# A hybrid mixer and mixture-of-experts layer: context tokens loaded earlier, a fixed expert order, late experts added into the residual stream, choices summed from the last blocks on

## The chip, the cores and the metric

The kernel runs on one core of a Trainium2 chip. The metric is the device time of one execution in microseconds (us); the time before is the median of three runs. A core has a matrix engine (TensorE, PE in the rows), a vector engine (DVE), an activation engine (ACT), a general one (POOL), a sequencer that only issues transfers (SP), and 16 DMA engines between the chip's memory (HBM) and the on-chip memory.

## The reference

One layer over 512 latent tokens of width 1024 with 256 context tokens ahead of them: a modulated RMSNorm, one projection, latent attention beside a recurrent block, an output projection, and then the part in which most of the time goes, a mixture of 64 experts. Each token picks 8 of them.

```python
def routed_experts(h, eidx, w, exp_w_gate, exp_w_up, exp_w_down):
    ...
    def body(acc, blk):
        tok_b, w_b, e_b = blk
        y = swiglu(h[tok_b], exp_w_gate[e_b], exp_w_up[e_b], exp_w_down[e_b])
        return acc.at[tok_b].add(y * w_b[:, None]), None
    ...
h_lat = modulate(rmsnorm(x, norm_mix_g[l]), sh1, sc1)
h_ctx = modulate(rmsnorm(ctx, norm_mix_g[l]), csh1, csc1)
...
x = x + g1 * (y_lat @ w_out[l])
...
x = x + g2 * (routed_experts(f_lat, ...) + swiglu(f_lat, sh_w_gate, sh_w_up, sh_w_down))
return rmsnorm(x, final_norm_g)
```

All is in float32. An expert has gate and up weights of 1024x256 and down weights of 256x1024, 1 MiB each; all 64 are used.

## The kernel before

**Prologue (to about 70 us).** SP issues the loads of this stage in the order of the code: the latent tokens (`load_x`, 4 of 512 KB), the key-value columns of the input projection (`wkv`), the first two modulation weights (`load_wm1(0)`), the context tokens (2 of 512 KB), the query columns (`wq`), and more weights. Each token tile is squared on ACT (line 295), gets its reciprocal root on DVE (lines 152 to 162, nine small operations) and is scaled there (line 299), then PE transposes it (`pt`, line 326) and DVE or ACT copies the result out. The modulation's rows come from PE (`pm`, line 311), and the first projection (`pkv`, line 362) needs the transposed tokens, modulated and split into a high and a low part (`hH`, `hL`).

**Recurrent block, attention (to about 332 us), output projection.** After the modulation rows are saved (`mrd<-modrow`) and two parts of the output weights are loaded (`wor`), SP has nothing to issue until attention is done.

**Routing and shared expert (332 to 440 us).** PE and DVE compute the router's logits, each token's 8 choices, and the place of every (token, choice) row in its expert's list. Beside that PE works off the shared expert in four token tiles: `sgu` (gate and up), `smul` (DVE), `sdn` (transposes `pst`, down products `psd`, then two DVE operations with `g2b` and the residual `x1`, and a store into the buffer `acc` in HBM). A scheduler sets the order of this stage by priorities.

**Expert blocks (440 to 1043 us).** The experts have ranks by the number of their tokens, and each rank has a capacity in units of 32 rows, 183 units in all. The list `order` (built at line 1090 on by a rule with `NTAIL` and `LEAD`) is cut into 46 blocks of up to 128 rows, so that one block can hold units of several experts. A block is a chain: `stage_sel` and `stage_gather` (three to four blocks ahead: its token rows, by an indirect DMA of POOL), `stage_trans` (PE `tr`, a copy `hT`), `stage_gu` (PE `gu`, 7 us), `stage_at`, `stage_down` (PE `dn`, 3.7 us, in a PSUM tile of which there is one; then `y` on DVE, line 1406, and an indirect DMA of POOL that scatters the rows into `yd`, a buffer in HBM with one row for each token and choice). PE's order here is written by hand: `gu` of a block, `tr` of the next, `at`, `dn`.

The weights come by SP: `load_upto` issues gate, up and down of the n-th expert in the list when the last block of the expert six places ahead is done, since there are six slots for each (`g0` to `g5` for gate and up, `d0` to `d5` for down); at most `OUTST` = 3 loads are in flight. Before the routing is known only the first `NF` = 3 experts can be loaded.

**End (1043 to 1113 us).** A loop over experts that overflow their capacity (no pass here) begins and ends with all engines waiting for each other. Then `fgb` (a gain) and 16 loads `yl<-yd` of 1 MB each bring the 8 choices of all tokens back. For each of four token tiles PE adds four choices (`fs`, with an identity matrix), DVE adds the other four and then PE's sum to the residual in `xs` (lines 1550 and 1551), ACT squares (`jk`), a root follows, and the scaled tile is stored. `fsum`, `fsq`, `frs` and `fout` are these steps.

## Time and profile before

| | |
|---|---|
| median of 3 runs | 1115.37 us (1114.18 to 1116.23) |
| the profiled execution | 1114.81 us |
| its span, first to last instruction | 1112.8 us |
| mean granted clock of TensorE | 0.962 |
| busy: PE / DVE / ACT / POOL | 996.2 / 484.3 / 255.7 / 223.4 us |
| HBM read / written | 293.31 / 30.29 MB |

The profile is one execution. Busy times do not count waits; a row of the timeline shows in brackets how long its engine stood idle before it and what ended that. The clock of TensorE is given as a share of its full 2.4 GHz. Numbers of a load or of a queue are of that queue alone; the DMA share of a window is that of all 16 engines.

### The profile page before, as it was taken

To read this page: it belongs to the slowest core of one execution; us is meant where nothing else is said; L and a number is where in the kernel's file an instruction comes from. 1 tells how busy PE (TensorE), PEld (TensorE's weight loads), DVE (VectorE), ACT (ScalarE), POOL (GpSimd) and SP (SyncE) were. 2 spreads that over 40 slices of the span, in tenths; PEclk is the share of its full clock that TensorE was granted. 3 is DMA by queue.
4 is the path that set the end of the run, shared out by engine and by line. 5 is a ranking of instruction groups with operands and counts; after the bars stand their busy time and mean duration, and the time that the engine had idled before them with its cause. 6 is when DMAs were issued, how large, how long until landed. Compare 5 with 4: busy or idle time off the path is not lost. (4 is left out here: it accounts for less than half of the span.)

```text
span 1112.8 us, 17435 instructions
## 1 busy us (share of the span) xinstructions
PE 996.2 (90%) x6813; PEld 515.6 (46%) x6813; DVE 484.3 (44%) x1064; ACT 255.7 (23%) x468; POOL 223.4 (20%) x219
## 2 busy tenths in 40 slices
PE   3899989799989998999999999999999999995482
PEld 2687654567779853443443344333333333331131
DVE  5527594988765865223222232222322223220065
ACT  3433545756661210011000110000100001000011
POOL 3382341346100001111111111111111111110001
PEclk9899999889999999999999999999999999997797
DMA  9834644200009543999999898989879999989694
GB/s 294 266 96 154 206 161 133 77 1 1 1 2 365 226 195 132 416 394 417 419 409 360 333 390 346 395 323 399 339 289 401 399 413 414 399 319 414 251 421 186
DMA packets 75404, 310.34 MB, mean 279 GB/s; under 512 B 12747, under 2 KB 31234, under 8 KB 48442
## 3 DMA queue, kind: packets, MB, share of 16 engines
q1 hardware_dynamic: 60412, 271.79, 63.2%
q0 software_dynamic: 13936, 34.26, 8.1%
q10 hardware_dynamic: 974, 3.17, 0.8%
q8 instruction: 54, 0.88, 0.3%
q14 instruction: 28, 0.23, 0.1%
HBM read 293.31 MB, written 30.29 MB: 291 GB/s over the span
## 5 line engine op out<-in xcount | busy, mean ns | idle before, releaser
L1382 PE MATMUL gu<-wgu,hT 128*32 128x512 f32 (+2 forms) x2160 | 333.0, 597 | 11.1 <-DMA wgu<-in_exp_w_up_dram 10.4
L1382 PEld LDWEIGHTS gu<-wgu,hT 128*32 128x32 f32 (+2 forms) x2160 | 105.4, 120 | 230.2 <-issue 225.9
L1403 PE MATMUL dn<-wd,aT 128*32 128x512 f32 (+2 forms) x1080 | 169.1, 596 | 16.6 <-ACT aT L124 15.4
L1385 DVE TENSOR_TENSOR act<-act,gu 128x256 f32<-128x256 f32 (+1 forms) x46 | 19.4, 421 | 297.8 <-ACT act L1384 297.8
L1384 ACT ACTIVATE act<-gu 128x256 f32<-128x256 f32 (+1 forms) x46 | 17.7, 385 | 511.7 <-PE gu L1382 511.7
L1332 POOL DMA_INDIRECT hg<-h2d,bix x46 | 47.6, 1034 | 425.9 <-issue 310.4
L1406 DVE SCALAR_TENSOR_TENSOR y<-dn,bw,g2b 128x1024 f32<-128x1024 f32 (+1 forms) x46 | 59.0, 1283 | 138.2 <-PE dn L1403 138.2
L1403 PEld LDWEIGHTS dn<-wd,aT 128*32 128x32 f32 (+2 forms) x1080 | 48.7, 119 | 100.8 <-issue 78.8
L1407 POOL DMA_INDIRECT yd<-y,biy x46 | 46.8, 1017 | 191.9 <-DVE y L1406 182.5
L1370 PEld LDWEIGHTS tr<-ident,hg 128*128 128x128 f32 (+1 forms) x368 | 39.9, 141 | 37.1 <-issue 34.1
L1370 PE MATMUL tr<-ident,hg 128*128 128x128 f32 (+1 forms) x368 | 49.7, 278 | 1.3 <-DVE tb L1084 1.3
L1548 PE MATMUL fs<-yl,ident 128*128 128x512 f32 x64 | 32.1, 654 | 20.3 <-DMA yl<-yd 18.1
L829 PE MATMUL pTr<-ident,P 128*128 128x128 f32 x192 | 30.7, 300 | 9.8 <-DVE P L820 7.7
L1306 DVE TENSOR_TENSOR sv<-iot,posR 128x256 bf16<-128x256 f32 (+3 forms) x93 | 37.1, 411 | 0.0
L812 DVE TENSOR_REDUCE nm<-pS 128x1 f32<-128x768 f32 x32 | 30.3, 951 | 11.2 <-PE pS L810 10.8
L124 ACT COPY PT<-pTr 128x384 f32<-128x384 f32 x64 | 28.0, 482 | 29.0 <-PE pTr L829 28.7
L124 ACT COPY hT<-tr 128x512 f32<-128x512 f32 (+1 forms) x46 | 26.9, 584 | 34.0 <-PE tr L1370 32.5
L840 PE MATMUL po<-PT,vsb 128*64 128x128 f32 x384 | 30.8, 299 | 1.7 <-ACT PT L124 1.7
L454 PE MATMUL pmx<-wm,csil 128*32 128x512 f32 x128 | 31.9, 606 | 0.0
L124 DVE COPY hT<-tr 128x512 f32<-128x512 f32 (+1 forms) x46 | 31.3, 680 | 0.0
L1548 PEld LDWEIGHTS fs<-yl,ident 128*128 128x128 f32 x64 | 12.7, 208 | 39.8 <-DMA yl<-yd 20.4
L829 PEld LDWEIGHTS pTr<-ident,P 128*128 128x128 f32 x192 | 24.1, 153 | 14.8 <-issue 7.7
(473 smaller groups left out, 1472.9 us busy)
## 6 DMA issues: line engine op xcount, KB each, us to landing
wgu<-in_exp_w_gate_dram SPq DMA_DIRECT2D x64, 1024.0 KB
wgu<-in_exp_w_up_dram SPq DMA_DIRECT2D x64, 1024.0 KB
wd<-in_exp_w_down_dram SPq DMA_DIRECT2D x64, 1024.0 KB
...
```

The source lines that it names most:

```text
L124: (e.copy if e is ACT else e.tensor_copy)(dst, src)
L454: PE.matmul(pm[32 * g:32 * g + 32, :], csil[:, kk, :], wmp[n, g // 2][:, (g % 2) * 512:(g % 2 + 1) * 512], start=(kk == 0), stop=(kk == KT ...
L829: PE.transpose(p[:, j * P:(j + 1) * P], Pm[u][:, k * P:(k + 1) * P], ident)
L840: PE.matmul(po[i][64 * hh:64 * hh + 64, t * P:(t + 1) * P], vsb[:, k, 2 * i + hh, :], PTt[i, t, hh][:, k, :], start=(k == 0), stop=(k == N ...
L1306: DVE.tensor_tensor(sv[:, :, c:c + w], iot[:, u:u + w][:, None, :].to_broadcast([P, NT, w]), col_[:, :, None].to_broadcast([P, NT, w]), op ...
L1332: POOL.indirect_dma_start(out=b.hg[0:m], out_offset=None, in_=h2d, in_offset=bass.IndirectOffsetOnAxis(ap=b.ix[0:m, :1], axis=0), bounds_c ...
L1370: PE.transpose(p[:, i * m:(i + 1) * m], b.hg[0:m, (i0 + i) * P:(i0 + i + 1) * P], ident[0:m, 0:m])
L1382: PE.matmul(p[c:c + w, :], b.hT[:, k, c:c + w], wg[n][:, :, k, :], start=(k == 0), stop=(k == KT - 1))
L1403: PE.matmul(p[c:c + w, n0:n0 + 512], b.aT[:, k, c:c + w], wd_[n][:, k, n0:n0 + 512], start=(k == 0), stop=(k == 1))
L1406: DVE.scalar_tensor_tensor(y[0:m], p[0:m], b.w[0:m], g2b[0:m], op0=OP.mult, op1=OP.mult)
L1407: ins = POOL.indirect_dma_start(out=yd, out_offset=bass.IndirectOffsetOnAxis(ap=b.iy[0:m, :1], axis=0), in_=y[0:m], in_offset=None, bounds ...
L1548: PE.matmul(p[:, n0:n0 + 512], ident, yl[t, k][:, n0:n0 + 512], start=(k == 0), stop=(k == 3))
```

## The change

- The context tokens are loaded directly behind the latent tokens, and `wkv` comes behind the first modulation weights.
- The list of experts is a table, `ORDER`. The last `LATE` = 5 of them (full 128 rows each) have a block of their own. In the same number of blocks (46) the last two of before held units of four and of three experts.
- The rows of these five blocks aren't written into `yd` but added into `acc` by the DMA itself; `acc` has 128 rows more, into which rows without a token are sent (`spad`). `yd` (16.8 MB) and these rows (0.5 MB) are filled with zeros by five transfers behind the loads of `wor`.
- The shared expert's parts are in an order written out by hand, `sgu(2)` and `sgu(3)` among the routing's products. `x1` and `wgu_s` change their buffers, so that slot `g2` comes free after `sgu(3)`, and `load_upto(NW - 2)` stands right behind it.
- DVE's order is written by hand from the first expert block on.
- The 16 loads `yl<-yd` are issued as slots come free in the last blocks (`sum_loads`). The first five of DVE's additions stand between `y` of block 44 and that of block 45, the rest behind the last `y`; PE adds four choices of the token tiles 1 to 3 (`fs`, in the tiles of `dn`, `tr` and `gu`). After the loop `acc` is loaded (`ya`, 4 of 512 KB) and added once for each token tile.

The diff, cut to its core (the removed `yload` issued the 16 loads behind the loop):

```diff
--- before.py
+++ after.py
@@ -75,9 +75,15 @@
...
-NTAIL = 8
...
+ORDER = [61, 62, 63, 35, 60, 48, 52, 21, 43, 38, 9, 50, 34, 2, 46, 28,
...
+LATE = 5
 OUTST = 3
...
 L0 = 2
...
@@ -112,7 +118,7 @@
...
+    acc = dram.tile([S + P, D], F32, name="acc")
...
@@ -264,7 +270,7 @@
...
-    wkv = load_win(C_KV, 160)
+    load_x(ctx[0], 2)
     wm1 = {}
...
@@ -274,7 +280,7 @@
...
     load_wm1(0)
-    load_x(ctx[0], 2)
+    wkv = load_win(C_KV, 160)
     wq = load_win(0, 256)
     for c in range(1, 4):
         load_wm1(c)
@@ -782,6 +788,12 @@
...
+    zt = modrow.rearrange("p a b -> p (a b)")
+    POOL.memset(zt, 0.0)
+    SP.dma_start(acc[S:S + P, :], zt)
+    for t in range(NT):
+        SP.dma_start(yd.rearrange("(t p k) f -> t p k f", p=P, k=TOPK)[t], zt[:, None, :].to_broadcast([P, TOPK, D]))
...
@@ -933,7 +945,7 @@
...
-    x1 = pW1.tile([P, NT, D], F32, tag="g2", name="x1")
+    x1 = pW1.tile([P, NT, D], F32, tag="g4", name="x1")
...
@@ -958,7 +970,7 @@
...
-    wgu_s = pW1.tile([P, 2, KT, FF], F32, tag="g4", name="wgu_s")
+    wgu_s = pW1.tile([P, 2, KT, FF], F32, tag="g2", name="wgu_s")
...
@@ -1056,47 +1070,48 @@
...
-    @prio("sgu")
-    def sgu(t):
-        p = sgp[t] = psx("psg")
-        for k in range(KT):
+    def sgu(t, k0=0, k1=KT):
+        if k0 == 0:
+            sgp[t] = psx("psg")
+        p = sgp[t]
+        for k in range(k0, k1):
             PE.matmul(p, h2T[:, k, t * P:(t + 1) * P], wgu_s[:, :, k, :], start=(k == 0), stop=(k == KT - 1))
-        sga[t] = et("act", "sg")
+        if k1 < KT:
+            return
...
-    @prio("sdn")
-    def sdn(t):
+    sgT = {}
+    def sdt(t):
...
-        p = pw("psd")
-        for n in range(2):
...
+    def sdp(t):
+        tb = et("y", "tb")
+        x_ = x1[:, t]
+        for n0 in range(0, D, 512):
+            p = psx("psd")
             for k in range(2):
-                PE.matmul(p[:, n * 512:(n + 1) * 512], sgT[:, k, :], wd_s[:, k, n * 512:(n + 1) * 512],
-                          start=(k == 0), stop=(k == 1))
-        tb = et("y", "tb")
-        DVE.tensor_tensor(tb, p, g2b, op=OP.mult)
-        DVE.tensor_tensor(tb, tb, x1[:, t], op=OP.add)
-        ACT.dma_start(acc[t * P:(t + 1) * P, :], tb)
+                PE.matmul(p, sgT[t][:, k, :], wd_s[:, k, n0:n0 + 512], start=(k == 0), stop=(k == 1))
+            DVE.tensor_tensor(tb[:, n0:n0 + 512], p, g2b[:, n0:n0 + 512], op=OP.mult)
+        DVE.tensor_tensor(x_, tb, x_, op=OP.add)
+        ACT.dma_start(acc[t * P:(t + 1) * P, :], x_)
...
-    order = [E - NF + j for j in range(NF)]
...
-    lead = LEAD
-    while left:
-        r = left.pop(0 if lead <= 0 else -1)
-        order.append(r)
-        lead += caps[r] * 0.092 - (8.1 + caps[r] * 0.019)
-    order += range(E - NF - NTAIL, E - NF)
-    GS, NW = (5, 0, 1, 2, 3, 4), 6
+    order = ORDER
+    GS, DS, NW = (5, 0, 1, 2, 3, 4), (0, 1, 2, 3, 5, 4), 6
...
@@ -1123,10 +1138,14 @@
...
     for n, r in enumerate(order):
+        if n >= E - LATE:
+            assert caps[r] <= P
+            at = 0
         for u in range(0, caps[r], 32):
...
@@ -1142,11 +1161,13 @@
...
+    for b in blocks[-LATE:]:
+        b.late = True
...
-        loads += [(n, "g") for n in new] + [(n, "d") for n in new]
+        loads += [(n, w) for n in new for w in ("dg" if n == NF else "gd")]
...
@@ -1180,6 +1201,8 @@
...
     logits(2)
+    st_M = ExitStack()
+    st_M.enter_context(tc.manual_schedule(engines={mybir.EngineType.PE}))
     sgu(0)
...
@@ -1234,6 +1257,8 @@
...
+    smul(1)
+    sgu(2, 0, 4)
...
@@ -1269,12 +1294,16 @@
...
+    sgu(2, 4, 6)
...
+    sgu(2, 6, 8)
...
@@ -1325,8 +1354,12 @@
...
+        if b.late:
+            DVE.tensor_scalar(b.iy[0:m], tk[0:m], float(FAR), spad[0:m], op0=OP.add, op1=OP.min)
+        else:
...
@@ -1334,30 +1367,32 @@
...
     LA = 3
-    smul(1)
+    sgu(3)
+    st_O.close()
+    st_E2 = ExitStack()
+    pE2 = st_E2.enter_context(tc.tile_pool(name="pE2", bufs=1))
+    load_upto(NW - 2)
+    smul(2)
     stage_sel(blocks[0])
     stage_sel(blocks[1])
-    sdn(0)
-    sgu(2)
+    smul(3)
+    sdt(0)
     stage_gather(blocks[0], pn("ix0"))
-    smul(2)
-    sdn(1)
+    sdt(1)
+    sdp(0)
     stage_gather(blocks[1], pn("ix1"))
     stage_sel(blocks[2])
-    sgu(3)
-    load_upto(NW - 2)
-    smul(3)
+    sdt(2)
+    sdp(1)
     stage_gather(blocks[2], pn("ix2"))
-    sdn(2)
-    sdn(3)
-    st_O.close()
+    sdt(3)
+    sdp(2)
+    sdp(3)
...
@@ -1404,13 +1439,16 @@
...
         DVE.scalar_tensor_tensor(y[0:m], p[0:m], b.w[0:m], g2b[0:m], op0=OP.mult, op1=OP.mult)
+        if b.late:
+            POOL.indirect_dma_start(out=acc, out_offset=bass.IndirectOffsetOnAxis(ap=b.iy[0:m, :1], axis=0),
+                                    in_=y[0:m], in_offset=None, bounds_check=S + P - 1, oob_is_err=True, compute_op=OP.add)
...
@@ -1459,8 +1497,42 @@
...
+    st_M.enter_context(tc.manual_schedule(engines={mybir.EngineType.DVE}))
+    ydv = yd.rearrange("(t p k) f -> t p k f", p=P, k=TOPK)
+    pairs = [(t, k) for t in range(NT) for k in range(0, TOPK, 2)]
+    homes = [("d", E - 6)] + [(w, n) for n in range(E - 5, E) for w in "dgh"]
+    yl, rest, place = {}, list(zip(pairs, homes)), {}
+    xs = None
+    def sum_loads(i):
+        nonlocal xs
+        if xs is None and i >= last[E - 6]:
...
+            (t, k), (w, n) = rest.pop(0)
...
+            ins = SP.dma_start(z, ydv[t, :, k:k + 2, :]).ins
+            for y_ in yw:
+                after(ins, y_, "rows of all blocks but the last")
+            yl[t, k] = z
+    def add_pair(t, k, first):
+        x_ = xs[:, t]
+        for j in range(2):
+            if first and j == 0:
+                DVE.tensor_tensor(x_, yl[t, k][:, 0, :], yl[t, k][:, 1, :], op=OP.add)
+            elif not first:
+                DVE.tensor_tensor(x_, x_, yl[t, k][:, j, :], op=OP.add)
...
@@ -1476,14 +1548,31 @@
...
+        if not loads:
+            sum_loads(i)
+        if i == NB - 2:
+            for k in (0, 2, 4):
+                add_pair(0, k, k == 0)
         if i in (10, 12, 14, 16):
             got = next(table)
...
+    for t in range(1, NT):
+        if t == 1:
+            p = pse.tile([P, D], F32, tag="dn", name="fs", bufs=1)
+            fs = [p[:, 0:512], p[:, 512:1024]]
+        else:
+            fs = [pse.tile([P, 512], F32, tag=("gu", "tr")[t % 2], name="fs", bufs=2) for _ in range(2)]
+        for k in range(4):
+            for h in range(2):
+                PE.matmul(fs[h], ident, yl[t, k - k % 2][:, k % 2, h * 512:(h + 1) * 512], start=(k == 0), stop=(k == 3))
+        add_pair(t, 4, True)
+        add_pair(t, 6, False)
+        for h in range(2):
+            x_ = xs[:, t, h * 512:(h + 1) * 512]
+            DVE.tensor_tensor(x_, x_, fs[h], op=OP.add)
     st_M.close()
-
-    xs = pW1.tile([P, NT, D], F32, tag=f"g{GS[(E - 6) % NW]}", name="xs")
-    for t in range(NT):
-        SP.dma_start(xs[:, t], acc[t * P:(t + 1) * P, :])
     n_ov = nc.values_load(nov[0:1, 0:1], min_val=0, max_val=NOV)
...
@@ -1520,35 +1606,14 @@
...
-    def yload(t, k0, n, buf):
...
+    n = E - 5
+    ya = (pW0 if GS[n % NW] < 2 else pW1 if GS[n % NW] < 5 else pW2).tile([P, NT, D], F32, tag=f"g{GS[n % NW]}", name="ya")
+    for t in range(NT):
+        SP.dma_start(ya[:, t], acc[t * P:(t + 1) * P, :])
     @prio("fsum")
     def fsum(t):
-        p = psf.tile([P, D], F32, tag="fs", name="fs", bufs=2)
-        for n0 in range(0, D, 512):
-            for k in range(4):
-                PE.matmul(p[:, n0:n0 + 512], ident, yl[t, k][:, n0:n0 + 512], start=(k == 0), stop=(k == 3))
-        for k in range(4, TOPK):
-            DVE.tensor_tensor(xs[:, t], xs[:, t], yl[t, k], op=OP.add)
-        DVE.tensor_tensor(xs[:, t], xs[:, t], p, op=OP.add)
+        DVE.tensor_tensor(xs[:, t], xs[:, t], ya[:, t], op=OP.add)
...
```

What this does to the instructions, at three places. First SP's issues in the prologue, from the latent tokens on. Before:

```order
L256 DMA xz<-in_x_dram 128x1024 x4
L264 DMA win<-in_w_in_dram 128x8x160
L273 DMA wm_136<-in_w_mod_dram 128x8x256
L273 DMA wm_138<-in_w_mod_dram 128x8x256
L256 DMA xz<-in_ctx_dram 128x1024 x2
L264 DMA win<-in_w_in_dram 128x8x256
L273 DMA wm_145<-in_w_mod_dram 128x8x256
```

And now:

```order
L262 DMA xz<-in_x_dram 128x1024 x4
L262 DMA xz<-in_ctx_dram 128x1024 x2
L279 DMA wm_137<-in_w_mod_dram 128x8x256
L279 DMA wm_139<-in_w_mod_dram 128x8x256
L270 DMA win<-in_w_in_dram 128x8x160
L270 DMA win<-in_w_in_dram 128x8x256
L279 DMA wm_145<-in_w_mod_dram 128x8x256
```

`xz<-in_ctx_dram` went up by three rows, and `wkv` (128x8x160) down by three.

Second PE, from the routing to the first expert block (`psg` are the products of `sgu`, `pst` and `psd` those of the shared expert's second half, `ptr` and `ppr` belong to the routing, `tr` begins block 0). Before, the last rows ahead of block 0:

```order
L1075 MATMUL pst<-ident,sg 128x128
L1063 MATMUL psg<-wgu_s,h2T 128x512
L1075 MATMUL pst<-ident,sg 128x128 x2
L1081 MATMUL psd<-wd_s,sgT 128x512 x4
L1063 MATMUL psg<-wgu_s,h2T 128x512 x2
L1081 MATMUL psd<-wd_s,sgT 128x512 x4
L1063 MATMUL psg<-wgu_s,h2T 128x512 x2
L1075 MATMUL pst<-ident,sg 128x128 x2
L1081 MATMUL psd<-wd_s,sgT 128x512 x4
L1370 MATMUL tr<-ident,hg 128x128 x8
```

And now, rows that end ahead of the first selection of token rows (`ix`):

```order
L1078 MATMUL psg<-wgu_s,h2T 128x512 x2
L1302 MATMUL ptr<-ident,eq 64x128 x4
L1302 MATMUL ptr<-ident,se 64x128 x4
L1078 MATMUL psg<-wgu_s,h2T 128x512 x2
L1309 MATMUL ppr<-perm,sT 128x64 x8
L1078 MATMUL psg<-wgu_s,h2T 128x512 x8
L1096 MATMUL pst<-ident,sg 128x128 x2
```

The last products of `psg` stood among the second half, three rows ahead of block 0; they now stand ahead of the first `pst`.

Third DVE, from the last block but one on. Before, up to the loop:

```order
L1406 SCALAR_TENSOR_TENSOR y<-dn,bw,g2b 128x1024
L1385 TENSOR_TENSOR act<-act,gu 128x256
L124 COPY hT<-tr 128x384
L1406 SCALAR_TENSOR_TENSOR y<-dn,bw,g2b 128x1024
L1385 TENSOR_TENSOR act<-act,gu 96x256
L1406 SCALAR_TENSOR_TENSOR y<-dn,bw,g2b 96x1024
L1489 TENSOR_LOAD nov
```

And now (line 1441 is `y`, line 1420 `act`), up to the additions of token tile 2; those of tile 3 and the loop follow:

```order
L130 COPY hT<-tr 128x512
L1441 SCALAR_TENSOR_TENSOR y<-dn,bw,g2b 128x1024
L1532 TENSOR_TENSOR xs<-yl 128x1024
L1534 TENSOR_TENSOR xs<-xs,yl 128x1024 x4
L1420 TENSOR_TENSOR act<-act,gu 128x256
L1441 SCALAR_TENSOR_TENSOR y<-dn,bw,g2b 128x1024
L1534 TENSOR_TENSOR xs<-xs,yl 128x1024 x2
L1532 TENSOR_TENSOR xs<-yl 128x1024
L1534 TENSOR_TENSOR xs<-xs,yl 128x1024 x2
L1574 TENSOR_TENSOR xs<-xs,fs 128x512 x2
L1532 TENSOR_TENSOR xs<-yl 128x1024
```

The additions of choices, which stood behind the loop, stand ahead of it, five of them ahead of the last `y`; a single addition of `ya` for each token tile is left behind the loop.

## Rows read from the trace of the kernel before

**Rows 1.** Waits of TensorE over the span: line, releaser: us, times, longest us

```profile
PE fs L1548 <- DMA yl<-yd: 18.1, 5, 13.4
PE dn L1403 <- ACT aT L124: 15.4, 46, 0.6
PE pt L326 <- DVE xz L299: 11.5, 3, 4.6
PE gu L1382 <- DMA wgu<-in_exp_w_up_dram: 10.4, 4, 3.6
PE pTr L829 <- DVE ccol L1419: 2.1, 1, 2.1
```

**Rows 2.** Timeline, prologue, SP, DVE, PE: start, us, engine, line, operation [idle before]

```profile
7.79 0.43 SPq L264 DMA_DIRECT2D win<-in_w_in_dram  x1
11.83 2.63 SPq L256 DMA_DIRECT2D xz<-in_ctx_dram  x2
32.18 1.42 DVE L299 TENSOR_SCALAR xz<-xz,rstd 128x1024 f32<-128x1024 f32 x2
33.08 2.73 PE L326 MATMUL pt<-ident,xz 128*128 128x128 f32 x10 [4.64 <-DVE xz L299]
```

**Rows 3.** Timeline, SP around attention

```profile
196.84 1.91 SPq L784 DMA_DIRECT2D wor<-in_w_out_dram  x2
332.84 0.34 SPq L943 DMA_DIRECT2D g1b<-mrd  x1
```

**Rows 4.** Windows, routing: us, busy by engine (x), PEclk, DMA share, GB/s

```profile
405.00:420.00 15.00, 13.92 (x66) 7.08 (x65) 9.78 (x28) 1.82 (x4) 0.00 (x0) 1.00 0.00 0
420.00:440.00 20.00, 16.98 (x57) 7.82 (x55) 11.81 (x23) 1.50 (x4) 4.02 (x3) 1.00 0.32 114
```

**Rows 5.** Timeline, PE, from the shared expert's end into blocks 0 and 1

```profile
439.18 1.09 PE L1370 MATMUL tr<-ident,hg 128*128 128x128 f32 x8 [1.32 <-DVE tb L1084]
441.04 8.82 PE L1382 MATMUL gu<-wgu,hT 128*128 128x512 f32 x16 [0.77 <-DVE hT L124]
455.72 6.60 PE L1382 MATMUL gu<-wgu,hT 128*128 128x512 f32 x15
```

**Rows 6.** Timeline, DVE, line 1406: start of y in blocks 0, 43, 44, 45

```profile
455.49 1.28 DVE L1406 SCALAR_TENSOR_TENSOR y<-dn,bw,g2b 128x1024 f32<-128x1024 f32 x1 [2.77 <-PE dn L1403]
999.10 1.28 DVE L1406 SCALAR_TENSOR_TENSOR y<-dn,bw,g2b 128x1024 f32<-128x1024 f32 x1 [4.22 <-PE dn L1403]
1015.67 1.28 DVE L1406 SCALAR_TENSOR_TENSOR y<-dn,bw,g2b 128x1024 f32<-128x1024 f32 x1 [6.47 <-PE dn L1403]
1042.74 1.28 DVE L1406 SCALAR_TENSOR_TENSOR y<-dn,bw,g2b 96x1024 f32<-96x1024 f32 x1 [4.69 <-PE dn L1403]
```

**Rows 7.** Windows, expert blocks; then the page's row of POOL's DMA queue

```profile
700.00:800.00 100.00, 97.29 (x942) 35.10 (x942) 27.61 (x81) 9.96 (x24) 16.22 (x16) 1.00 0.93 367
1000.00:1030.00 30.00, 18.01 (x110) 5.15 (x113) 2.56 (x4) 1.24 (x3) 1.96 (x2) 0.80 1.01 415
q0 software_dynamic: 13936, 34.26, 8.1%
```

**Rows 8.** Timeline, after the last y: POOL, SP, PE, DVE, ACT

```profile
1044.29 0.95 POOL L1407 DMA_INDIRECT yd<-y,biy  x1 [26.09 <-DVE y L1406]
1049.20 0.34 SPq L1518 DMA_DIRECT2D fgb<-in_final_norm_g_dram  x1
1056.10 11.96 PE L1548 MATMUL fs<-yl,ident 128*128 128x512 f32 x20 [13.42 <-DMA yl<-yd]
1068.57 5.42 PE L1548 MATMUL fs<-yl,ident 128*128 128x512 f32 x12 [0.51 <-DMA yl<-yd]
1092.58 5.00 DVE L1550 TENSOR_TENSOR xs<-xs,yl 128x1024 f32<-128x1024 f32 x4
1097.68 1.22 DVE L1551 TENSOR_TENSOR xs<-xs,fs 128x1024 f32<-128x1024 f32 x1
1102.99 1.15 ACT L1573 ACTIVATE xs<-xs,rf 128x1024 f32<-128x1024 f32 x1 [2.49 <-DVE rf L1566]
```

82 lines of the change are left out of this document (32 added, 50 removed), and 3 rows, old and new, of the table ORDER.

## The prediction, made before the run

> **What bounds the kernel now.** I read TensorE's waits over the whole span first [rows 1]: they add up to little, and the larger ones have a place each. The sum of choices waits 18.1 us for its loads, the down products 15.4 us for a copy that no part of the change touches (46 times a third of a microsecond), the transposes of the prologue 11.5 us for a scaling, the gate products 10.4 us for weights. Then the windows of the expert blocks [rows 7]: PE is busy for 97.29 of 100 us, while the DMA engines have a share of 0.93. So the long middle is PE's, with the loads close behind. Then the starts of `y` [rows 6], one for each block: from block 0 to block 43 they are (999.10 - 455.49) / 43 = 12.64 us apart; the last two are 16.57 and 27.07 us apart. There the DMA share is 1.01 at 415 GB/s, and PE works 18.01 of 30 us [rows 7]: loads bind, since seven experts of few rows (21 MB of weights) fall into two blocks. Last, from the start of the last `y` to the end of the span, 1112.8 - 1042.74 = 70.06 us pass, with loads, additions and stores in turn [rows 8]. So the change is to be judged in five places: prologue, attention, routing, blocks, end.
>
> **A, prologue.** PE waits 4.64 us for the scaled context tokens [rows 2], whose two loads are issued at 11.83, behind `wkv` at 7.79 and two modulation weights. With these loads first, that wait is gone. The modulation weights now have 1 MB of context ahead of them in the place of 0.65 MB of `wkv` (128x8x160 floats), so the modulated latent tokens come 0.4 MB later, about 1 us at 415 GB/s [rows 7]. `wkv` lands about where the context did, and has to be split before the first projection; I take 0.6 us for that. 4.6 - 1.0 - 0.6 = 3.0 us gained. Ends: 4.6 gained, or 2 lost (the whole MB of context, 2.5 us, ahead of the modulation, with nothing gained). Behind it PE is full, so a gain here is passed on.
>
> **B, attention.** DVE's operations on the overflow table, which cost PE 2.1 us in attention [rows 1], move into the blocks, where DVE is busy 27.61 of 100 us [rows 7]. The clearing on POOL is one operation in a stretch in which POOL is mostly idle; I allow 0.6 us. The five transfers that write zeros, 16.8 + 0.5 = 17.3 MB, are issued behind `wor` at about 199 us; SP issues nothing more until 332.84 [rows 3], so they have 134 us and need 129 GB/s of DMA engines that are otherwise idle. Taken as hidden: 1.5 us gained, ends 2 gained and 1 lost. What it costs if that cover is too short is a rival below.
>
> **C, routing to block 0.** In the last stretch ahead of block 0 PE waits 1.32 us for DVE's residual addition and 0.77 us for the copy of block 0, and the first gate products take 8.82 us, where 15 of the 16 of the next block take 6.60 [rows 5] (the whole about 7.04). That is 1.3 + 0.8 + 1.8 = 3.9 us that an order with filled gaps can take back. The hand-written order puts `sgu(2)` and `sgu(3)` where PE would wait for the routing, and so leaves less to fill the gap ahead of the first selection; I keep 3.0. Ends: 5 gained, 1 lost. The first `y` then starts at 455.49 - 7.5 = 448.0.
>
> **D, the blocks.** 45 intervals of 12.64 us are 568.8 us, where 1042.74 - 455.49 = 587.25 us pass now [rows 6]: 18.4 us less, if weights never bind. Whether they bind I worked out by a queue walk: 61 experts with three loads of 1.05 MB at 2.6 us (403 GB/s, a little below the 415 of the saturated window), 34.26 MB of gathers and scatters [rows 7] spread over 46 blocks (0.74 MB or 2.2 us each), a load not before its slot is free, three in flight. For the order of before the walk loses 19 us, all in the last two blocks; the trace shows 16.57 + 27.07 - 2 x 12.64 = 18.4. For the table it loses 6 us, in blocks 17 and 36, where slots come free late; at 2.55 us a load none, at 2.65 us 13. I take 3: D = 18.4 - 3 = 15.4 us gained, ends 20 (blocks a little tighter) and 5. Two things help that the walk has: slot `g2` comes free after `sgu(3)`, so that the DMA engines, which move nothing from 405 to 420 and have a share of 0.32 until 440 [rows 4], start on the fourth expert earlier; and the last five blocks need one expert each. The 16 loads of choices now fall into these blocks: 16.8 MB are 40 us at 415 GB/s, in five blocks of 63 us that have no weights left to load. The last `y` starts at 448.0 + 568.8 + 3 = 1019.8.
>
> **E, the end.** After the last `y` (1.28 us) PE has the sums of three token tiles, 48 records. The first of these needs the PSUM tile that `y` reads. At the upper clock 12 records take 5.42 us [rows 8], 0.45 each: 21.7 us. DVE has in the same time 2 + 3 x 3 additions of 1024 columns at 1.25 and 6 halves, about 17.5 us, and so is covered; the last half, 0.6 us, is not. 1.28 + 21.7 + 0.6 = 23.6. The loop's barrier and the first issue behind it: 2.0 (`fgb` is issued at 1049.20, 4.0 us after POOL was done with its scatter at 1045.24, and most of that is the scatter landing). Then `fgb` (0.5 MB) and four times 0.5 MB of `acc`: from the issue of `fgb` to PE's first sum, behind 1.57 MB, it took 1056.10 - 1049.20 = 6.9 us; 1.05 MB more at 415 GB/s is 2.5, so 9.4. One addition, 1.22. From the end of the last addition, 1098.90, to the end of the span 13.9 us, which stay; and since DVE then does the roots of two tiles and scales two tiles at once, 3.5 more. 23.6 + 2.0 + 9.4 + 1.2 + 13.9 + 3.5 = 53.6, against 70.06: 16.5 us gained. Ends: 21 (no mutual delay of the tiles) and 0 (the 48 records at the clock's lower level, where 20 records at first took 11.96 [rows 8], some 40 us instead of 21.7).
>
> **Sum.** 3.0 + 1.5 + 3.0 + 15.4 + 16.5 = 39.4 us. The profiled execution took 1114.81, so 1075.4; the median lies 0.56 above it: **1076 us**.
>
> **The rivals.** (1) *The loads bind.* At 2.7 us a load, or with 3 us of DMA time a block in place of 2.2, the walk loses 20 to 32 us in blocks 13 to 39 in place of 3: 1093 to 1105. For it: shares of 0.93 to 1.01 [rows 7]. Against it: the same walk with the smaller numbers meets the waits of before. Chance 0.12. The Trainium skill, "DMA: Bandwidth & Descriptors", section "Specifications", names about 358 GB/s as what a core gets from its HBM. By that alone the 226 MB of weights (61 x 3.15), gathers and scatters (34.26) would take 630 us from about 425 on, and 1076 would be about 1118, no gain; the window at 415 GB/s [rows 7] speaks against it, and I give such a result 0.01. (2) *The late additions are a chain.* Each transfer that adds into `acc` has to wait for the one before; if one takes longer than a block of 12.64 us, they pile up, and the loop's barrier waits for the last. The nearest row is a plain scatter, issued at 1044.29 and over before 1049.20 [rows 8], under 5 us. At 20 us the chain ends 5 x 20 = 100 us after the first late `y` at 1019.8 - 4 x 12.64 = 969.2, at 1069 in place of 1043: 26 us more, 1102. Chance 0.04. The skill's same page, section "Rules for kernel authors", says why the chain is needed: an adding DMA reads its target and writes it later, and another write in between is lost. (3) *The zeros outlast attention*, the case on the other side. All that follows at 332.84 needs the same 16 engines: `g1b`, tokens and output weights. Above 129 GB/s nothing is lost; each us behind 332.84 costs up to one; 39.4 us are used up at a finish at 372, that is 17.3 MB in 173 us, 100 GB/s. At 80 GB/s they take 216 us, end at 415, and the time is 1076 + 82 = 1158. Against it: 415 GB/s in a saturated stretch [rows 7]; for it only that no row shows a write of this size from a broadcast source. Chance 0.04. (4) *The context load gains nothing:* A is 0 and the time 1079, inside the range.
>
> **How the numbers follow.** Forecast 0.79, loads 0.12, chain 0.04, zeros 0.04, no gain 0.01. The forecast's own ends, not all at once, give 1058 to 1092. The range holds these and the near half of the loads' case: 1060 to 1096; what lies outside is about 0.2. A measurement of this kernel tells about 0.2% from no change. Faster by more than that: 0.79 + 0.12 + 0.04 = 0.95; the same 0.01; slower 0.04.
>
> **What would show it.** A: TensorE's wait for line 299's scaling falls from 11.5 to under 8. B: the DMA windows between 200 and 250 show the writes, and SP's first issue behind attention is not followed by a longer wait of PE. C: the first `y` near 448. D: starts of `y` 12.6 apart up to the last, and waits for weights of some us near blocks 17 and 36; if the walk is wrong, more of these. E: `fs` behind the last `y` without a wait for loads, and 53 us from that `y` to the end. The prediction is wrong if the intervals between blocks grow to 13 us or more, since 45 of them multiply it.

## The result, and the profile after

The changed kernel took **1076.68 us** (median of 4 runs, 1073.87 to 1082.02) against 1115.8 before (4 runs): a ratio of 0.9653, with a 95% interval from 0.9608 to 0.9698. The forecast was 1076. The profiled execution took 1078.44, its span is 1076.7, so 36.1 us less than the span of before.

The sum agrees because the two large terms held; the small ones in front of them did not. In the two profiled executions the span falls into the parts of the prediction like this (the gains add up to 36.0 us, where 39.4 were forecast):

| part | before | after | gained | predicted |
|---|---|---|---|---|
| A, to the store of the modulation rows (SP) | 196.12 | 196.30 | -0.2 | 3.0 |
| B, from there to the first issue behind attention | 136.72 | 133.77 | 2.9 | 1.5 |
| C, from there to the first `y` | 122.65 | 122.11 | 0.5 | 3.0 |
| D, first `y` to last `y` | 587.25 | 571.76 | 15.5 | 15.4 |
| E, last `y` to the end | 70.06 | 52.76 | 17.3 | 16.5 |

TensorE's waits over the whole span (line, releaser: us, times, longest us) answer to [rows 1]. The wait of `fs` for its loads is gone, that of `gu` for weights has shrunk from 10.4 to 1.4, and that of the prologue's transposes from 11.5 to 7.4, as the prediction asked of A; and yet A brought nothing.

```profile
PE dn L1438 <- ACT aT L130: 16.0, 46, 0.5
PE pt L332 <- DVE xz L305: 7.4, 5, 2.2
PE gu L1417 <- DMA wgu<-in_exp_w_up_dram: 1.4, 1, 1.4
PE fs L1569 <- DVE y L1441: 1.4, 1, 1.4
```

**A.** PE's timeline in the prologue (start, us, operation, idle before), and two windows (us, then busy us and count of PE, PEld, DVE, ACT, POOL, then PEclk, DMA share, GB/s):

```profile
30.80 0.47 PE L368 MATMUL pkv<-hH,wh 128*128 128x512 f32 x1 [0.32 <-ACT hH L394]
33.40 0.58 PE L370 MATMUL pkv<-hH,wh 128*128 128x256 f32 x1 [0.95 <-ACT hH L394]
35.77 0.80 PE L368 MATMUL pkv<-hL,wh 128*128 128x512 f32 x1 [1.00 <-DVE hL L398]
36.58 0.63 PE L368 MATMUL pkv<-hH,wl 128*128 128x512 f32 x1
...
32.00:36.00 4.00, 2.05 (x8) 1.06 (x9) 3.71 (x3) 2.54 (x4) 3.98 (x2) 0.65 1.10 348
36.00:40.00 4.00, 4.00 (x19) 3.06 (x23) 0.96 (x1) 0.00 (x0) 0.00 (x0) 0.50 1.10 348
```

Before, the first of these products and one of the same shape as the last:

```profile
37.98 0.61 PE L362 MATMUL pkv<-hH,wh 128*128 128x512 f32 x1
39.25 0.39 PE L362 MATMUL pkv<-hH,wl 128*128 128x512 f32 x1
```

The first projection (`pkv`) starts at 30.80 where it started at 37.98, seven us earlier. But the projection falls into a stretch in which PE waits for ACT and DVE to split the tokens (0.95 and 1.00 us), and which has a granted clock of 0.65 and then 0.50, its lower level of 1.2 GHz. There a product of 512 columns takes 0.63 us where the same took 0.39 before, at 39 us. Of the seven us 1.4 are left at the first product of the recurrent stage (`pp`, at 72.26 in place of 73.65), and these too are lost by the store of the modulation rows at 196.30. The section on the prediction takes this up.

**B.** SP's issues and the windows of attention, which answer to [rows 3]:

```profile
200.37 23.77 SPq L796 DMA_DIRECT2D yd<-modrow  x4
330.07 0.34 SPq L955 DMA_DIRECT2D g1b<-mrd  x1
...
207.00:240.00 33.00, 28.00 (x166) 21.35 (x165) 31.86 (x43) 20.61 (x40) 20.81 (x12) 0.92 1.02 421
240.00:260.00 20.00, 18.78 (x115) 13.90 (x113) 15.94 (x23) 12.52 (x27) 7.79 (x5) 0.79 0.35 142
```

The zeros go out at 421 GB/s and are done by about 247 (a share of 0.35 of the window from 240 to 260), 83 us ahead of the first load behind attention.

**D.** The starts of `y` on DVE that answer to [rows 6], with blocks 16 and 17 (the second and third row):

```profile
452.18 1.28 DVE L1441 SCALAR_TENSOR_TENSOR y<-dn,bw,g2b 128x1024 f32<-128x1024 f32 x1 [2.46 <-PE dn L1438]
654.53 1.28 DVE L1441 SCALAR_TENSOR_TENSOR y<-dn,bw,g2b 128x1024 f32<-128x1024 f32 x1 [2.60 <-PE dn L1438]
670.26 1.28 DVE L1441 SCALAR_TENSOR_TENSOR y<-dn,bw,g2b 128x1024 f32<-128x1024 f32 x1 [2.69 <-PE dn L1438]
1011.34 1.28 DVE L1441 SCALAR_TENSOR_TENSOR y<-dn,bw,g2b 128x1024 f32<-128x1024 f32 x1 [4.22 <-PE dn L1438]
1023.94 1.28 DVE L1441 SCALAR_TENSOR_TENSOR y<-dn,bw,g2b 128x1024 f32<-128x1024 f32 x1 [4.82 <-PE dn L1438]
```

The intervals are 12.5 to 13.0 us to the very end. One is longer, 15.73 us, that of block 17, which the queue walk had named; block 36, the other one it had named, has 12.75. PE's rows in block 17:

```profile
655.01 1.07 PE L1417 MATMUL gu<-wgu,hT 128*64 128x512 f32 x2
657.46 7.05 PE L1417 MATMUL gu<-wgu,hT 128*64 128x512 f32 x30 [1.38 <-DMA wgu<-in_exp_w_up_dram]
```

Its gate products end 9.5 us after the first began, in place of 7.1, with a wait for weights among them: 2.4 us. The other 0.64 us are products of the overflow table (`pot`, from 654.37 to 655.01), which stand in that block before the change too, where its interval is 13.32 us.

**E.** Behind the last `y`: PE, DVE, SP, and a window of it, to be read beside [rows 8].

```profile
987.13 38.07 SPq L1523 DMA_DIRECT2D yl<-yd  x16
1025.28 20.87 PE L1569 MATMUL fs<-yl,ident 128*128 128x512 f32 x48 [1.38 <-DVE y L1441]
1043.14 1.23 DVE L1532 TENSOR_TENSOR xs<-yl 128x1024 f32<-128x1024 f32 x1 [3.13 <-DMA yl<-yd]
1045.69 2.48 DVE L1534 TENSOR_TENSOR xs<-xs,yl 128x1024 f32<-128x1024 f32 x2 [1.33 <-DMA yl<-yd]
1048.28 1.29 DVE L1574 TENSOR_TENSOR xs<-xs,fs 128x512 f32<-128x512 f32 x2
1051.40 1.94 SPq L1612 DMA_DIRECT2D ya<-acc  x4
1056.72 2.51 DVE L1616 TENSOR_TENSOR xs<-xs,ya 128x1024 f32<-128x1024 f32 x2 [7.16 <-DMA ya<-acc]
1062.75 4.57 DVE L1640 SCALAR_TENSOR_TENSOR xs<-xs,rf,fgb 128x1024 f32<-128x1024 f32 x2
...
1030.00:1040.00 10.00, 10.00 (x25) 4.39 (x24) 7.47 (x9) 0.00 (x0) 0.00 (x0) 1.00 1.03 371
```

PE's 48 records take 20.87 us (21.7 predicted) and end at 1046.15. But DVE waits 3.13 and 1.33 us for the last loads of choices, and its last addition ends at 1049.57: the DMA engines, busy all the time (1.03 at 371 GB/s), end last, not PE. SP began to issue these loads at 987.13 and had issued the last of the 16 at about 1025, behind the last `dn`. The part up to the loop is 25.6 us (23.6 predicted), that behind it is shorter (27.1, 30.0 predicted).

### The profile page after: what moved, and what is told of

Read it like the earlier page. It is cut to its first block, busy times and chain, and to the rows that moved or that the text cites. A ratio compares the mean times of both kernels' runs of the same rounds, so it can differ in the third digit from the quotient of the medians.

```text
span 1076.7 us, 16080 instructions
## 1 busy us (share of the span) xinstructions
PE 978.7 (91%) x6125; PEld 523.5 (49%) x6125; DVE 489.7 (45%) x1062; ACT 255.1 (24%) x468; POOL 234.6 (22%) x221
## 5 line engine op out<-in xcount | busy, mean ns | idle before, releaser
L1417 PE MATMUL gu<-wgu,hT 128*32 128x512 f32 (+3 forms) x1776 | 326.5, 594 | 2.1 <-DMA wgu<-in_exp_w_up_dram 1.4
L1417 PEld LDWEIGHTS gu<-wgu,hT 128*32 128x32 f32 (+3 forms) x1776 | 111.7, 127 | 209.3 <-issue 208.2
L1438 PE MATMUL dn<-wd,aT 128*32 128x512 f32 (+3 forms) x888 | 168.5, 597 | 16.0 <-ACT aT L130 16.0
L1365 POOL DMA_INDIRECT hg<-h2d,bix x46 | 50.4, 1095 | 418.9 <-issue 305.1
L1438 PEld LDWEIGHTS dn<-wd,aT 128*32 128x32 f32 (+3 forms) x888 | 52.1, 127 | 96.8 <-issue 76.2
L1446 POOL DMA_INDIRECT yd<-y,biy x41 | 41.2, 1004 | 138.3 <-DVE y L1441 125.0
L1335 DVE TENSOR_TENSOR sv<-iot,posR 128x256 bf16<-128x256 f32 (+3 forms) x86 | 34.1, 435 | 0.0
L1078 PE MATMUL psg<-wgu_s,h2T 128*128 128x512 f32 x64 | 30.6, 625 | 0.0
L826 ACT ACTIVATE P<-pS,nm 128x768 f32<-128x768 f32 x32 | 29.1, 909 | 4.8 <-DVE nm L824 4.6
```

The costliest lines, as they stand in the source:

```text
L1078: PE.matmul(p, h2T[:, k, t * P:(t + 1) * P], wgu_s[:, :, k, :], start=(k == 0), stop=(k == KT - 1))
L1335: DVE.tensor_tensor(sv[:, :, c:c + w], iot[:, u:u + w][:, None, :].to_broadcast([P, NT, w]), col_[:, :, None].to_broadcast([P, NT, w]), op ...
L1365: POOL.indirect_dma_start(out=b.hg[0:m], out_offset=None, in_=h2d, in_offset=bass.IndirectOffsetOnAxis(ap=b.ix[0:m, :1], axis=0), bounds_c ...
L1417: PE.matmul(p[c:c + w, :], b.hT[:, k, c:c + w], wg[n][:, :, k, :], start=(k == 0), stop=(k == KT - 1))
L1438: PE.matmul(p[c:c + w, n0:n0 + 512], b.aT[:, k, c:c + w], wd_[n][:, k, n0:n0 + 512], start=(k == 0), stop=(k == 1))
L1446: ins = POOL.indirect_dma_start(out=yd, out_offset=bass.IndirectOffsetOnAxis(ap=b.iy[0:m, :1], axis=0), in_=y[0:m], in_offset=None, bounds ...
```

## Experiments

Each run stands beside runs of the kernel before on the same chip; in the first and third group the changed kernel ran beside it as well, in the second it did not. The executions of the changed kernel spread over 6 to 11 us within a group (1071 to 1085 over all), those of before over 4 to 6 (1113 to 1120); differences of 2 to 3 us between medians are therefore read from positions in the traces and not from the times.

### First group: the prologue, the start of the loads, the last scaling

The base, unchanged:

> The changed kernel once more, as the base for the runs beside it on the same chip. Both theories: 1077 us, within 3; start of the first y 452, of the last 1024, 52.8 us from there to the end.

Measured: 1076.22 (6 runs, 1073.66 to 1084.93). The execution that was profiled was its longest (span 1083.2): D took 575.0 us, with intervals of 13.1 to 14.9 us in blocks 13, 15, 17, 36 and 39, and B 136.9.

The context loads back:

```diff
-    load_x(ctx[0], 2)
+    wkv = load_win(C_KV, 160)
     wm1 = {}
 ...
     load_wm1(0)
-    wkv = load_win(C_KV, 160)
+    load_x(ctx[0], 2)
```

> The changed kernel with the context loads back in their old place, behind the first modulation weights. Theory 1 (the gain of the context move is given back before attention: what ends the recurrent stage is not PE's prologue): the wait for the scaled context grows back by about 4 us, PE is busy about 3.8 us less before 40 us, but the store of the modulation rows on SP stays within 0.5 us of 196.3 and the time within 2 us of the base. Rival (the 3.0 us of the prediction are passed on): the store comes 3 us later, and the time is 3 us longer.

Measured: 1078.64 (1075.12 to 1079.65), 2.4 above the base and inside its spread. The first projection is back at 37.44, the first `pp` at 73.41; the store of the modulation rows is at 195.85, where the rival has 199. Theory 1 holds for the store; the time lies 0.4 us beyond the 2 us that it allowed, which this spread does not decide. (`c3` below has the move alone.)

Without the early call that issues expert weights:

```diff
     pE2 = st_E2.enter_context(tc.tile_pool(name="pE2", bufs=1))
-    load_upto(NW - 2)
     smul(2)
```

> The changed kernel without the early call that issues expert weights behind the shared expert's third tile, so that the fourth expert's loads come with the call ahead of block 0 (about 440 in place of 409 to 421). Theory 1 (the middle is carried by the early start of the loads): the queue walk gives 5 to 13 us more waiting for weights, in blocks 12, 13 and 17: 1082 to 1090. Rival (the order of the table alone does it, and PE binds anyway): within 2 us of the base.

Measured: 1074.88. This told nothing: in its trace the loads are issued at 421.46, as in the first profile of the changed kernel (421.34). The order of SP's issues had not changed with the call's place. What the load waits for is its slot; that is the run `b3` below.

The last scaling on DVE alone:

```diff
-    ... "fx0": "D", "fx1": "D", "fx2": "P", "fx3": "P" ...
+    ... "fx0": "D", "fx1": "D", "fx2": "D", "fx3": "D" ...
```

> The changed kernel with the last scaling of all four token tiles on DVE, where tiles 2 and 3 were multiplied on POOL and scaled on ACT. Theory 1 (DVE and POOL slow each other when both multiply: 2.28 us in place of 1.28 on DVE, 3.2 in place of 2.34 on POOL): DVE's scalings take 1.28 us each again, the last one starts about 1067, and the end comes 3 us earlier: 1074. Rival (DVE's slow operations there have another cause): scalings of 2.3 us stay, and the time is within 1 us of the base or up to 2 us longer, since DVE has two more.

Measured: 1073.06 (1068.07 to 1077.01), 3.2 below the base. DVE's timeline at the end of this kernel; the last row covers two scalings:

```profile
1064.86 0.25 DVE L1629 TENSOR_TENSOR fr<-fr 128x1 f32<-128x1 f32 x2
1065.44 2.48 DVE L1640 SCALAR_TENSOR_TENSOR xs<-xs,rf,fgb 128x1024 f32<-128x1024 f32 x2
```

Two scalings take 2.48 us where they took 4.57 in the changed kernel beside POOL's products, and the small operation on `fr` 0.25 where it took 1.75. From the first addition of `ya` to the end of the last scaling 12.1 us pass (1055.85 to 1067.92) where 15.5 passed (1056.72 to 1072.2). Theory 1 holds.

### Second group: the table, the overlap, the slots, the zeros

The table in the kernel before:

```diff
-    order = [E - NF + j for j in range(NF)]
-    ... (the rule with NTAIL and LEAD)
+    order = ORDER
```

> The kernel before with the list of experts replaced by the table, nothing else: no blocks of their own for the last five experts, no earlier loads, choices summed behind the loop as before. Theory 1 (the blocks' gain comes from the order of the experts, since no two blocks are full of small experts at the end): the two long intervals at the end, 16.6 and 27.1 us, vanish, waits for weights of some us come in blocks 13 to 17, and the time falls by 8 to 17 us: 1098 to 1107. Rival (the order alone is not enough, since the loads start at 440 and the walk then loses 16 to 23 us in blocks 12 to 40): within 4 us of the kernel before, 1112 to 1118.

Measured: 1109.13 (1106.71 to 1113.49), a ratio to before of 0.9937 (0.9921 to 0.9953), 6.8 us: between the 8 to 17 us of theory 1 and the 4 us of the rival. The long intervals at the end are gone, but blocks 13 and 40 take 19.5 and 20.8 us in their place, and first to last `y` is 584.56 (587.25 before). Waits of PE for weights, and the last window:

```profile
PE gu L1378 <- DMA wgu<-in_exp_w_up_dram: 9.0, 3, 4.6
1000.00:1040.00 40.00, 35.87 (x249) 12.29 (x238) 7.46 (x9) 3.18 (x8) 3.00 (x3) 1.00 0.24 90
```

The DMA engines have a share of 0.24 in the last window, so the weights are all there by then: the waiting lies earlier, where loads bind.

Loads and early additions written behind the last block:

```diff
-        if not loads:
-            sum_loads(i)
-        if i == NB - 2:
+        if i == NB - 1:
+            sum_loads(i)
             for k in (0, 2, 4):
                 add_pair(0, k, k == 0)
```

> The changed kernel with all 16 loads of choices issued behind block 45, and the five early additions behind them. Theory 1 (the end's gain is the overlap of these 16.8 MB with the last blocks): 40 us of loads at 415 GB/s start at about 1022 and end about 1064, the additions end 2 to 4 us later in place of at 1049, and the time grows by 16 to 19 us: 1093 to 1096. Rival (the gain comes from fewer steps behind the loop, and the loads would be hidden by the sums anyway): under 8 us more.

Measured: 1079.73; E is 52.3 us, as in the changed kernel (52.8). SP still issued the loads from 981 on, as in the changed kernel (987), so that this run moved only the five additions. In the trace they are worth nothing: DVE waits for the last loads anyway, and its additions end 25.1 us behind the last `y` (25.6 in the changed kernel). The time is 3 us above the changed kernel's first median, with no run of that kernel beside it, so an effect of this size on the time is not excluded. The overlap itself was tested in `c1`.

`x1` and `wgu_s` in their old buffers:

```diff
-    x1 = pW1.tile([P, NT, D], F32, tag="g4", name="x1")
+    x1 = pW1.tile([P, NT, D], F32, tag="g2", name="x1")
 ...
-    wgu_s = pW1.tile([P, 2, KT, FF], F32, tag="g2", name="wgu_s")
+    wgu_s = pW1.tile([P, 2, KT, FF], F32, tag="g4", name="wgu_s")
```

> The changed kernel with x1 and the shared expert's gate and up weights in their old buffers, so that the slot of the fourth expert comes free when the shared expert is done, at about 437, and not at 421. (Without the early call alone the loads were still issued at 421, so that run said nothing on this.) Theory 1 (the early start of the loads carries the middle): SP's next gate load comes at about 438 in place of 421, the waits in blocks 12 to 17 grow by 5 to 13 us: 1081 to 1090. Rival (the table alone does it): the loads come late, and the time stays within 2 us of 1076.

Measured: 1084.48 (1082.86 to 1087.31), 8 to 11 us above the changed kernel's medians. SP's issue of the fourth expert's gate weights, and PE's wait for weights in the blocks:

```profile
440.73 0.33 SPq L1119 DMA_DIRECT2D wgu<-in_exp_w_gate_dram  x1
PE gu L1417 <- DMA wgu<-in_exp_w_up_dram: 5.1, 2, 4.1
```

The load comes at 440.73 in place of 421.34. Blocks 12 and 13 take 14.5 and 19.3 us, and first to last `y` is 579.1. Theory 1 holds: the early start carries about half of D (579.1 against 571.8, of a gain of 15.5).

Five times the zeros:

```diff
-    for t in range(NT):
+    for t in [t for _ in range(5) for t in range(NT)]:
         SP.dma_start(yd.rearrange(...)[t], zt[:, None, :].to_broadcast([P, TOPK, D]))
```

> The changed kernel with the choice buffer filled with zeros five times, 84 MB in place of 17. Theory 1 (a fill that ends within attention is free, and one that outlasts it delays the loads behind it one for one): at the measured 421 GB/s it takes 201 us and ends at about 401 in place of 241, the output weights and tokens that follow at 332 wait for it, and the time grows by 50 to 75 us: 1126 to 1151, slower than before the change. Rival (later loads share the engines with the fill and are served beside it): under 30 us more.

Measured: 1145.75, slower than before (1.0269, 1.0240 to 1.0297) and 69 us above the changed kernel. SP's issue of the zeros, PE's longest wait, and a window behind the time at which attention ended before:

```profile
198.78 185.59 SPq L796 DMA_DIRECT2D yd<-modrow  x20
PE pwo L1014 <- DVE tm L1020: 69.7, 1, 69.7
380.00:400.00 20.00, 0.00 (x0) 0.00 (x0) 0.00 (x0) 0.00 (x0) 0.00 (x0) 0.50 1.02 422
```

SP itself is held by these issues for 185.59 us and issues `g1b` at 384.47; the loads behind then wait for what is queued, and PE stands for 69.7 us. The first `y` is at 520.6 (452.2). So the prediction's slower case is real, and its price is one for one: the fill lasts until about 400, 68 us behind the 332 at which SP's next load stood, and the time grows by 69. The fill of the change has a margin of 83 us.

### Third group: the overlap again, a better end, the context move alone

The base:

> The changed kernel once more, as the base for the runs beside it. Both theories: 1076.5, within 2.

Measured: 1073.36 (1071.4 to 1077.85), 1 us below the range expected for it and 3 below the base of the first group.

Every load of choices made to wait (the edit of `b2`, and):

```diff
-            POOL.indirect_dma_start(out=acc, ..., compute_op=OP.add)
+            lw = POOL.indirect_dma_start(out=acc, ..., compute_op=OP.add).ins
+            lws.append(lw)
             return
 ...
                 after(ins, y_, "rows of all blocks but the last")
+            after(ins, lws[-1], "behind the last block")
```

> The changed kernel with every load of choices made to wait for the last block's addition into acc, and the five early additions behind them. (In the run with the loads only written later in the code, SP still issued them from 981 on, so that run showed the early additions alone.) Theory 1 (the end's gain is the overlap of these 16.8 MB with the last five blocks): the loads start about 6 us behind the last y, take 41 us at 415 GB/s, additions and the loop follow: the end grows from 52.8 to 72 to 80 us, 1096 to 1104. Rival (the gain comes from fewer steps behind the loads, and the additions run beside them as before): under 8 us more.

Measured: 1105.53 (1104.38 to 1108.19), 32 us above the base and just over the range of theory 1; E is 81.7 us. The last addition into `acc` and the loads:

```profile
1026.60 1.58 POOL L1443 DMA_INDIRECT acc<-y,biy  x1 [11.14 <-DVE y L1441]
1032.89 22.66 SPq L1525 DMA_DIRECT2D yl<-yd  x16
```

So the overlap is worth about 31 us (81.7 against 50.8 in the base), more than the whole of E's gain. Without it the new end is longer than the old one (70.06): the sums end 54.3 us behind the last `y`, and the loop's barrier, the load of `acc`, one more addition, the scalings and the stores follow in 27.4 us, where before the steps of the four tiles ran beside the loads.

The better end:

```diff
-    ... "fx2": "P", "fx3": "P" ...
+    ... "fx2": "D", "fx3": "D" ...
 ...
+    fgb = et("hg", "fgb")
+    SP.dma_start(fgb, final_norm_g[None, :].to_broadcast([P, D]))
     n_ov = nc.values_load(nov[0:1, 0:1], min_val=0, max_val=NOV)
 ...
-    fgb = et("hg", "fgb")
-    SP.dma_start(fgb, final_norm_g[None, :].to_broadcast([P, D]))
```

> The changed kernel with the last scaling of all four tiles on DVE, and the load of the final gain ahead of the loop in place of behind it. Theory 1 (DVE and POOL slow each other there, and behind the loop the 0.5 MB of the gain pass ahead of acc): 3.4 us from the first, 1 to 1.3 us from the second: 1072. Rival (the first loads of acc are held by the time of a single transfer, not by the gain ahead of them): 1073, as with the scaling alone.

Measured: 1070.77 (1068.2 to 1076.3), 2.6 below the base of this group, no more than the scaling alone brought in the first group (3.2). It is the best of all kernels here (ratio to before 0.9591, 0.9571 to 0.9611). The first addition of `ya` starts 3.2 us after the issue of its load, where it took 5.3 in the changed kernel:

```profile
1053.97 1.75 SPq L1612 DMA_DIRECT2D ya<-acc  x4
1057.15 2.51 DVE L1616 TENSOR_TENSOR xs<-xs,ya 128x1024 f32<-128x1024 f32 x2 [4.64 <-DMA ya<-acc]
1061.08 1.22 DVE L1616 TENSOR_TENSOR xs<-xs,ya 128x1024 f32<-128x1024 f32 x1 [1.33 <-DMA ya<-acc]
```

DVE waits another 1.33 us for the third tile (the third row). From the end of DVE's additions of choices to the end of the span 22.1 us pass, against 23.4 with the scaling alone (`a4`): behind the sums the second edit brings 1.4 us, about the 1 to 1.3 of theory 1. But in this execution the sums themselves end 0.9 us later (26.2 us behind the last `y`, 25.3 in `a4`), and E is 48.3 us against 48.8. Whether the load of the gain, which SP now issues 2.5 us behind the last `y`, delays the last loads of choices, or whether this is spread, one execution does not tell; a net gain from the second edit is not shown.

The context move alone, in the kernel before:

> The kernel before with the context loads directly behind the latent ones and the key-value weights behind the first modulation weights, nothing else. Theory 1 (most of what the prologue gains is given back by the end of the recurrent stage): first projection about 7 us earlier (31 in place of 38), the first product of the recurrent stage 1.2 us earlier (72.4 in place of 73.6), the store of the modulation rows 0 to 1.2 us earlier, and the time within 2 us of the kernel before. Rival (3.0 us as predicted): the store at 193, and 1112 to 1113.

Its edit is that of `a2` the other way round. Measured: 1116.49 (11 runs) against 1116.04 (15 runs), a ratio of 1.0005 (0.9993 to 1.0017). PE's first projection and SP's store of the modulation rows:

```profile
30.75 0.76 PE L362 MATMUL pkv<-hH,wh 128*128 128x512 f32 x1
...
194.54 0.66 SPq L780 DMA_DIRECT2D mrd<-modrow  x1
```

The projection starts seven us earlier, at the half clock again (0.76 us for its first product). The first `pp` is at 72.19. By itself the context move makes no difference that can be measured; the interval leaves room for a gain of 0.8 us.

## Why the prediction was right, and where it was not

**A failed.** Its price of the lost wait was right (the prologue's transposes wait 4.1 us less), and `wkv` came early enough: POOL starts to split it at 22.79, 8 us ahead of the first projection. What failed is the sentence "Behind it PE is full, so a gain here is passed on". PE is busy from 40 us on in both kernels, but part of that is the same work at the lower clock, and 1.4 us are left at the first `pp`. What then happens to these 1.4 us shows when all 14 profiled executions are sorted by the granted clock of the window from 80 to 120 us, in which PE is busy all the time:

| context loads | clock 80 to 120 | first `pp` to the store | store of the modulation rows | executions |
|---|---|---|---|---|
| behind | 1.00 | 120.9 | 194.4 | `b1` |
| behind | 0.96 | 122.4 to 122.5 | 195.9 to 196.1 | before, `a2` |
| first | 0.96 | 122.3 to 122.7 | 194.5 to 195.0 | `a3`, `a4`, `b4`, `c3` |
| first | 0.91 | 124.0 to 124.1 | 195.4 to 196.3 | after, `a1`, `b2`, `b3`, `c0`, `c1`, `c2` |

What PE has gained at the first `pp` is kept up to the store at an equal clock: at 0.96 the context first is worth about 1.2 us. In seven of eleven executions the clock takes most of it back, 1.6 us of the stretch from `pp` to the store. So A is a term of 1.2 us, less about 1 where the clock is lower, where 3.0 stood.

**B was gained in one trace, and not for its reason.** The zeros are hidden, as said. But the wait of 2.1 us that B was to take away is still there. The prediction put it down to the overflow table, since the row names `ccol`. PE's transposes (`pTr`) wait there for DVE's scaling of `P`, which takes 2.81 us for 128x768 where the one before it, at 279.55, took 0.61; a write into `ccol` merely came last, at 284.09. Before the change:

```profile
281.34 2.81 DVE L820 TENSOR_SCALAR P<-P,nm 128x768 f32<-128x768 f32 x1
284.29 1.51 PE L829 MATMUL pTr<-ident,P 128*128 128x128 f32 x6 [2.08 <-DVE ccol L1419]
```

And after it, with POOL's last constant beside them:

```profile
279.88 2.98 DVE L832 TENSOR_SCALAR P<-P,nm 128x768 f32<-128x768 f32 x1
281.09 1.35 POOL L1005 MEMSET V<- 128x256 bf16 x1
283.01 0.84 PE L841 MATMUL pTr<-ident,P 128*128 128x128 f32 x6 [2.26 <-DVE P L832]
```

In both kernels POOL writes a row of constants (`jj` to `V`, from 275.65 to 282.44 in the second) while DVE scales. In `b4` POOL writes them only from 408.36 on, and there the same scaling takes 0.61 us (at 279.69) and the wait is gone. From the same product of `pS` (at 272.3 in `b4`, at 272.5 in the first profile) to the last product of attention `b4` needs 49.1 us and the first profile 51.4, both at a granted clock of 1.00. So, as far as one execution shows it, the price of some 2 us was right for this wait, and its cause, which the change does not touch, is POOL's work beside DVE's. Which of POOL's operations hold DVE is not shown: an earlier scaling, at 278.09, stands beside the first of these constants and takes 0.61 us.

B is nevertheless 133.8 us in the first profile, and 136.8 to 136.9 in eight other executions with this attention stage; in three with the old one it is 136.7 to 137.0. The 3 us go with the clock from 280 to 300 us, in which PE is busy for 17.7 to 17.9 of the 20 us: 1.00 in the first profile and in `b3` (133.7), 0.91 in the eleven others (`b4`, where SP is held, left out). That accounts for 1.8 of the 3 us at most. The mean over the whole stage does not tell them apart (0.94 in the first profile and in `c0`, where B is 136.8), so what makes the rest stays open. At the lower clock B gained nothing.

**C was too large, and its largest term was not a gap.** PE's wait ahead of block 0 fell from 1.32 to 0.78 us and the other stayed at 0.77. The first gate products took 7.13 us in place of 8.82, as forecast, but the 1.8 us that the prediction priced there were not what "an order with filled gaps can take back": they are the clock, which was 0.83 from 440 to 450 us before the change (0.17 of 10 us is 1.7) and is 1.00 after it. In the changed kernel the clock falls earlier in the same stage instead, in this profile and in six other executions:

```profile
439.41 7.13 PE L1417 MATMUL gu<-wgu,hT 128*128 128x512 f32 x16 [0.77 <-DVE hT L130]
440.00:450.00 10.00, 9.71 (x46) 4.90 (x45) 2.46 (x11) 1.32 (x3) 0.60 (x1) 1.00 0.54 200
395.00:420.00 25.00, 22.86 (x85) 11.43 (x84) 15.80 (x59) 1.83 (x4) 0.00 (x0) 0.93 0.33 126
```

The window of before:

```profile
440.00:450.00 10.00, 9.23 (x22) 4.08 (x21) 0.98 (x2) 0.70 (x2) 0.00 (x0) 0.83 0.89 349
```

Over the whole stage the mean clock is 0.99 in the three executions with the old order (C is 122.6 us) and in these seven (122.0 to 122.1), so at an equal clock the new order is worth 0.5 us. In three others (`a2`, `a3`, `a4`) the clock is 1.00 throughout, and C is 120.5. Waits of the old order for DVE went (1.2 and 1.1 us, at `pst` and `ix`), but the hand-written order waits 2.13 us for DVE ahead of the choice counts (`pcn`) and 1.1 at the router's logits, where none was, for want of products to fill them: the cost that the prediction named in words and priced at 0.9 us. The first `y`, forecast for 448.0, came at 452.2.

**D held, and mainly for its reason.** The experiments show what carries the 15.5: in the traces the table alone brings 2.7 (`b1`), the whole change without the early slot 8.2 (`b3`), with it 15.5; what the last five experts' own blocks bring by themselves was not run. The walk was also right that the order by itself does not do: `b1` loses 15.8 us against 45 equal intervals (584.56 - 568.8), in blocks 13 and 40. That D fits to 0.1 us is luck. The walk itself gave 6 us, in blocks 17 and 36; the 3 was chosen between that and none, and the 2.2 us it took for 0.74 MB of gathers and scatters in a block have no row (at 415 GB/s they are 1.8). Waiting for weights measured 2.4 us in this profile, and over ten executions of this block stage with the early slot D lies 0.8 to 6.2 us above 568.8 (569.6 in `a2` to 575.0 in `a1`).

**E held in size, in this trace by two errors that cancel.** PE's term was right (20.87 us), but here it does not end last: the loads of choices do. The prediction gave them "five blocks of 63 us that have no weights left to load", but the last weights are issued at 986.62, and only then do the loads of choices begin, with the DMA engines full until 1040. So the additions end 2.0 us later than said, and the steps behind the loop are 2.9 shorter. In five other executions (`a2`, `a3`, `b3`, `b4`, `c0`) the loads come in time: the additions end 22.9 to 23.2 us behind the last `y`, as forecast (23.6), and E is 50.5 to 50.8 us, some 3 us better than the forecast. The case that the clock would drop during PE's sums did not come: PEclk is 1.00 until 1050. (The 40 us given for that case are not what its row gives: 20 records in 11.96 us make 28.7 for 48.)

**The rivals.** Loads that bind: 2.4 us in this trace, and one to two more at several places in the longest execution (D 575.0 in place of 571.8), part of the spread of the changed kernel. The 358 GB/s of the Trainium skill, "DMA: Bandwidth & Descriptors", section "Specifications": not seen; the zeros move at 421 GB/s, the saturated blocks at 389 to 415. The chain of additions: one takes 6.3 us from POOL's issue to the release of SP's load in `c1`, half a block, and doesn't bind. The zeros: decided by `b4`. The context load that gains nothing: it was given no chance of its own, as lying inside the range, and it is close to what came.

**The sum.** That the forecast meets the median to 1 us is in part luck. In the first profile A, B and C brought 3.2 of the 7.5 us forecast, and in `c0` (span 1076.0) 1.1; there the five parts gained 0.6, -0.1, 0.6, 16.4 and 19.2 us, so that D and E make up for what the front lacks. One thing the comparison of times has that the spans do not: the medians differ by 39.1 us, the profiled spans by 36.1. The profiled execution of before lies 1.0 us below its median and that of the changed kernel 1.8 above.
